# A trunk layer on one core: three spacings in the attention's side work are changed by one tick each

## The chip, the cores and the metric

The kernel runs on one core of a Trainium2 chip. TensorE (PE) multiplies matrices, VectorE (DVE) and ScalarE (ACT) work element by element, GpSimd (POOL) does the same and issues transfers of its own, and SyncE (SP) issues most of the transfers from memory. Each engine runs its own instructions in the order in which the program lists them; an instruction that needs another engine's result waits for it, and everything behind it on its engine waits too.

The metric is the device time of one execution in microseconds. Three runs of the kernel before took 2701.99, 2710.27 and 2707.65 us: median 2707.65.

## What is computed

One layer for 512 tokens of width 2048, in float32. The part that the change touches is the attention of eight heads of 128, cut from the reference:

```python
q = rmsnorm(q.reshape(B, S, SB_HEADS, SB_HEAD_DIM), q_norm_g[i])
k = rmsnorm(k.reshape(B, S, SB_HEADS, SB_HEAD_DIM), k_norm_g[i])
...
    z = jnp.einsum('bhqd,bhkd->bhqk', qi, kf).astype(jnp.float32) * scale
    strict = key_pos[None, :] < q_pos[:, None]
    log_beta = jax.nn.log_sigmoid(z)
    log_1m = jnp.where(strict, jax.nn.log_sigmoid(-z), jnp.zeros_like(z))
    tail = lax.cumsum(log_1m, axis=3, reverse=True) - log_1m
    w = jnp.where(strict, jnp.exp(log_beta + tail), jnp.zeros_like(z))
    return jnp.einsum('bhqk,bhkd->bhqd', w.astype(vf.dtype), vf)
```

So each query attends to the keys before it with weights that come from running sums along the keys. Beside this, the layer has a spatial gating, gates, an output projection, a gated feed-forward part and an embedding step; all of them are large products with weights that are read from memory once.

## The kernel before, in words

**The large products.** The layer is one long stream of matrix products, cut into units. A weight tile is loaded by SP (L316, L318), one part of it is added onto the loaded tile by a transfer that POOL issues (L338), DVE forms sums (L350), ACT rounds the result to its high half (L334) and DVE takes the low half (L331). PE multiplies with these: L271 to L273 and L629. The results are collected by ACT (L685) and DVE (L688). Weights are prepared some groups ahead.

**The side work.** Attention's small steps are put between the units. Each is a generator; a function `tick` is called about twice in each group of a product's units, and at a tick the generators that are due go on to their next `yield`. `yield n` means: go on n ticks later. `beside(steps, first)` starts a generator `first` ticks from now (1 where nothing is said). A tick only says behind which unit an instruction stands at the earliest; the scheduler that lists the instructions of each engine decides the rest by what each of them depends on. The side work's results of PE lie in a pool of two banks ("small"), so a third one must wait until the first has been read.

**The rounds.** Heads are done two at a time, in four rounds (0 to 3). In each round the loop at the end forms the queries, the keys and the values (L1238 to L1241 start their side work) and then three or four gate tiles, in whose time the attention runs. In round 0 queries, keys and values are formed together. Two halves (h = 0, 1) are the two heads.

- `q_prep` (L984): for each half, transpose (`flip`, L959), squares (L966, ACT), mean (L974, DVE), power (L976, POOL), scale (L991, DVE), then, a `yield` later, the scaling `times` (L981, ACT, four instructions) and, two ticks later, a second transpose that ACT copies out (L998).
- `k_prep` (L1001): for each half, transpose, squares, mean and power by the same lines.
- `v_prep` (L1008): for each half, transpose and `times` (L981).
- `attention` (L1013): eight blocks of 128 keys, four for each head, the last ones having 512 queries. Scores and their logarithms (`stage_a`: L1034 on PE, L1036 to L1039 on ACT), masks (`stage_m`: L1043, L1045, L1047, L1054, L1055), splitting the sums in two (`stage_b`: L1058, `stage_c`: L1062 on DVE), then the closing step of a block, `stage_d`: two products with a triangle (L1068, L1069), the sums handed on (L1071), the exponent's argument (L1073, DVE), the exponential (L1074, ACT) and the mask (L1075, POOL). `finish` (L1084 on PE) multiplies the weights of all four blocks of a head with the values, copies the output (L1086), and after the second head stores it (L1088, SP).

Of the kernel before, what the change touches and what calls it, by code (L numbers as in the profile page):

```python
# [65 lines left out]
def hybrid_layer(  # L66
# [28 lines left out]
    def nm(s):  # L95
        return f"{s}_{next(names)}"
# [14 lines left out]
    class Arena:  # L111
# [5 lines left out]
        def take(self, n, how="low"):  # L117


            spots = []  # L120
            for start, size in self.holes:
                end = start + size
                if how == "place":
                    start = -(-start // (2 * PLACE)) * 2 * PLACE
                if end - start >= n:
                    if how == "high":
                        spots.append((-end, end - n))
                    elif how != "old":
                        spots.append((start, start))
                    else:  # L130
                        spots.extend((self.given[a // P : -(-(a + n) // P)].max(), a)
                                     for a in {*range(start, end - n + 1, 256), end - n})
            at = min(spots)[1]
            start, size = next(h for h in self.holes if h[0] <= at < h[0] + h[1])
            self.holes.remove((start, size))
            self.holes.extend(
                h for h in ((start, at - start), (at + n, start + size - at - n)) if h[1])
            return Block(self, at, n)

        def give(self, block):  # L140
            self.turns += 1
            self.given[block.start // P : -(-(block.start + block.n) // P)] = self.turns
            holes = sorted(self.holes + [(block.start, block.n)])
            self.holes = holes[:1]
            for s, n in holes[1:]:
                if sum(self.holes[-1]) == s:
                    self.holes[-1] = (self.holes[-1][0], self.holes[-1][1] + n)
                else:
                    self.holes.append((s, n))
# [42 lines left out]
    def after(n, fn):  # L192
        heapq.heappush(waiting, (clock[0] + n, next(names), fn))
# [55 lines left out]
    def beside(steps, first=1):  # L249


        def step():
            n = next(steps, None)
            if n is not None:
                after(n, step)

        after(first, step)
# [595 lines left out]
    def rms_tile():  # L853
        return tmp.tile([P, 8], F32, tag="rr", name=nm("rr"), bufs=4)
# [87 lines left out]
    def a_tiles():  # L942

        for tag, n in (("l", T), ("w0", T), ("w1", 3 * P), ("w2", 2 * P), ("w3", 2 * P),
                       ("first", 5 * P), ("k", 1024), ("v", 1024), ("zs", 1024)):
            att[tag] = take(n)
        for tag in ("zh", "zl"):
            att[tag] = parts.take(T, "high")

    def a_tile(tag, n=T, start=0):  # L950
        return att[tag].f(start, start + n)
# [3 lines left out]
    def flip(o):  # L955

        ps = small_bank()
        for t in range(NT):
            nc.tensor.transpose(ps[:, t * P : (t + 1) * P], o[:, t * P : (t + 1) * P], ident)  # L959
        return ps  # L960
# [9 lines left out]
    def token_rms(ps, r):  # L970

        norm1.row()
        ms = squares(ps)
        nc.vector.scalar_tensor_tensor(out=ms, in0=ms, scalar=1.0 / P, in1=eps_cols,  # L974
                                       op0=ALU.mult, op1=ALU.add)
        nc.gpsimd.tensor_tensor(out=r, in0=ms, in1=expo[:, :NT], op=ALU.pow)  # L976

    def times(dst, ps, r):
        for t in range(NT):
            s = slice(t * P, (t + 1) * P)  # L980
            nc.scalar.activation(dst[:, s], ps[:, s], AF.Copy, scale=r[:, t : t + 1])  # L981

    def q_prep(o, i):


        for h in range(2):
            yield 2
            ps = flip(o[:, h * T : (h + 1) * T])
            q, r = take(T), rms_tile()[:, :NT]
            token_rms(ps, r)  # L990
            nc.vector.tensor_scalar(out=r, in0=r, scalar1=float(P) ** -0.5, scalar2=None,  # L991
                                    op0=ALU.mult)
            yield 1
            times(q.f(), ps, r)
            yield 2
            if not h:
                y_b[i] = take(1024)
            nc.scalar.activation(y_b[i].f(h * T, (h + 1) * T), flip(q.f()), AF.Copy,  # L998
                                 scale=gcol[:, g_q : g_q + 1])
            give(q)  # L1000
# [7 lines left out]
    def v_prep(o, v):  # L1008
        for h in range(2):
            yield 2  # L1010
            times(v[:, h * T : (h + 1) * T], flip(o[:, h * T : (h + 1) * T]), norm1.cols)

    def attention(rnd, kT, rk, v):  # L1013
# [27 lines left out]
        def stage_m(h, j):  # L1041
            l, s, w = a_tile("l")[:, : (NT - j) * P], sums(j), weights(h, j)
            nc.vector.scalar_tensor_tensor(out=w, in0=s, scalar=0.0, in1=l,  # L1043
                                           op0=ALU.min, op1=ALU.subtract)
            nc.vector.scalar_tensor_tensor(out=s, in0=s, scalar=0.0, in1=l,  # L1045
                                           op0=ALU.max, op1=ALU.add)
            nc.gpsimd.affine_select(out=s[:, :P], in_=s[:, :P], pattern=[[1, P]],  # L1047
                                    compare_op=ALU.is_gt, fill=0.0, base=0,
                                    channel_multiplier=-1)


            if j < NT - 1:
                if j:
                    nc.gpsimd.tensor_copy(first(j), s[0:1])  # L1054
                nc.gpsimd.memset(s[0:1, :P], 0.0)  # L1055

        def stage_b(j):
            nc.scalar.activation(zh[:, : (NT - j) * P], sums(j), AF.Copy)  # L1058

        def stage_c(j):  # L1060
            n = (NT - j) * P
            in_turn(nc.vector.tensor_tensor(out=zl[:, :n], in0=sums(j), in1=att["zh"].f(0, n),  # L1062
                                            op=ALU.subtract))
# [16 lines left out]
        def finish(h):  # L1080
            y = small_bank()
            for j in range(NT):
                c = h * T + j * P
                nc.tensor.matmul(y[:, j * P :], v[:, c : c + P], state.pop((h, "w", j)),  # L1084
                                 start=j == 0, stop=j == NT - 1)
            nc.scalar.activation(qT[:, h * T : (h + 1) * T], y, AF.Copy)  # L1086
            if h == 1:
                nc.sync.dma_start(out=y_spill[rnd], in_=qT)  # L1088
                give(y_b[rnd])
                y_done["b", rnd] = True  # L1090
# [7 lines left out]
        for i, (h, j) in enumerate(blocks):  # L1098
            ahead = blocks[i + 1 : i + 3]
            stage_b(j)  # L1100
            yield 1
            if i == NT:
                finish(0)
            stage_c(j)
            if ahead:
                stage_m(*ahead[0])
            yield 1
            stage_d(h, j)
            if ahead[1:]:
                stage_a(*ahead[1])  # L1110
            yield 1
# [114 lines left out]
    for n, ((w, i), pr) in enumerate(zip(order, made())):  # L1226
        if n == 0:
            row1 = norm1.row()
            nc.vector.tensor_scalar(out=eps_cols, in0=norm1.mean, scalar1=EPS, scalar2=None,
                                    op0=ALU.mult)  # L1230
        if n == 0:
            a_tiles()
        o = pr.out(block(w, i) if n < 3 else None)
        if w == "q":
            beside(q_prep(o, i))
        elif w == "k":
            kT, rk = o, rms_tile()
            beside(k_prep(kT, rk))  # L1238
            beside(attention(i, kT, rk, a_tile("v", 1024)), 6)
        elif w == "v":  # L1240
            beside(v_prep(o, a_tile("v", 1024)))  # L1241
        elif w == "s":
            scaled(o, row1)
            nc.scalar.activation(o, o, AF.Gelu_apprx_tanh)
            beside(sgu_v(i, o))
        elif w == "u":
            scaled(o, row1)
            nc.scalar.activation(o, o, AF.Gelu_apprx_tanh)
            nc.vector.tensor_tensor(out=y_a[i].f(), in0=o, in1=y_a[i].f(), op=ALU.mult)
            y_done["a", i] = True  # L1250
        else:
            d = tc.dram_tile([P, 1024], F32, name=nm("gsp"))
            nc.sync.dma_start(out=d, in_=o)
            gate_spill[w, i] = d
# [80 lines left out]
    for m in range(KH):  # L1335
        o = pair(fs, last=m == KH - 1, plain=m == 0, doubled=7).out()
# [36 lines left out]
    for j in range(KU):  # L1373
# [22 lines left out]
        else:  # L1396
            o = pair(gs, plain=j == 0).out()
# [90 lines left out]
```

## Time and profile before

| | |
|---|---|
| median of three runs | 2707.65 us (2701.99 to 2710.27) |
| the profiled execution's span | 2701.9 us |
| TensorE busy | 99% of the span |
| VectorE, ScalarE, GpSimd busy | 79%, 51%, 17% |
| memory traffic | 195 GB/s over the span |

The profile is of one execution, with all times in microseconds from the start of its span. In the list of waits a row names the engine that stood still and at what, then the engine and line that released it, then the total, how often, and the longest. In the timeline a row gives start, duration, engine, line and form, and in square brackets how long the engine was idle before it and what ended that. Matmuls overlap each other in the array, so the durations of neighbours overlap; the distance between two starts is what one takes from the stream. The clock that TensorE was granted is given as a share of full speed.

### The profile page before, as it was taken

Reading aid. Unit: us, or ns where it says so; the run is one execution under the profiler, and the core shown is the slowest. Engines: PE = TensorE matmul, PEld = TensorE weight load, DVE = VectorE, ACT = ScalarE, POOL = GpSimd, SP = SyncE. Lnnn points to the kernel's source line nnn. Section 1 sums busy time; section 2 is a strip of 40 time slices with the busy share of each in tenths; the row PEclk is TensorE's granted clock in tenths of the full one; section 3 lists DMA queues with packets and bytes.
Section 4 is the critical chain, followed back from the end, with each engine's and each line's share of the span. In section 5 each row is a group of like instructions: output and inputs, shape, how many; then the busy total and the mean of one; then the engine's idle time right before and its main releaser. Section 6 shows DMA issues by size and latency. Waiting matters only on the chain.

```text
span 2701.9 us, 43167 instructions
## 1 busy us (share of the span) xinstructions
PE 2668.1 (99%) x15875; PEld 2354.6 (87%) x15875; DVE 2147.0 (79%) x3621; ACT 1367.3 (51%) x2143; POOL 459.0 (17%) x543
## 2 busy tenths in 40 slices
PE   8999999999999999999999999999999999999999
PEld 6888888989998889988888888888888999988898
DVE  7687878787887566688988888888889667688776
ACT  7656565655554343374444444444445344453543
POOL 0232323232220000001111111111111111110110
PEclk9999999999999999999999999999999999999999
DMA  7677777777776467678888888888887668688784
GB/s 224 156 185 175 181 173 186 170 187 197 177 186 197 140 173 200 173 219 211 212 212 202 200 203 205 201 198 210 195 210 206 181 167 262 184 249 236 218 243 133
DMA packets 303268, 529.40 MB, mean 196 GB/s; under 512 B 25680, under 2 KB 162896, under 8 KB 303056
## 3 DMA queue, kind: packets, MB, share of 16 engines
q1 hardware_dynamic: 242304, 426.22, 49.9%
q0 software_dynamic: 60752, 100.43, 23.8%
q8 instruction: 124, 2.03, 0.3%
q14 instruction: 88, 0.72, 0.1%
HBM read 479.36 MB, written 47.19 MB: 195 GB/s over the span
## 4 chain that ended last, share of the span: by engine, by line
PE 88%; DVE 5%; DMA 2%; ACT 2%; issue 1%; POOL 1%; SPq 0%; DVEq 0%; ACTq 0%; POOLq 0%
PE ps L629 39%; PE ps L272 14%; PE ps L273 14%; PE ps L271 14%; PE small L629 4%; DVE wlo L331 2%; DVE out L688 1%; PE small L1084 1%; PE small L959 1%; ACT whi L334 1%; DMA wholes<-w_in 0%; DMA wholes<-w_first 0%; DVE wholes L350 0%; PE small L1034 0%; DVE parts L267 0%
## 5 line engine op out<-in xcount | busy, mean ns | idle before, releaser
L334 ACT ACTIVATE whi<-wholes 128x512 fp32r<-128x512 f32 (+4 forms) x950 | 857.6, 917 | 838.3 <-DVE wholes L350 261.9
L629 PE MATMUL ps<-parts,whi 128*128 128x512 f32 x3384 | 1134.8, 398 | 0.3 <-DVE p L688 0.3
L331 DVE TENSOR_TENSOR wlo<-wholes,whi 128x512 fp32r<-128x512 f32 (+4 forms) x950 | 962.4, 1046 | 101.0 <-ACT whi L334 100.5
L271 PE MATMUL ps<-parts,whi 128*128 128x256 f32 (+1 forms) x2675 | 855.1, 323 | 15.7 <-ACT parts L266 9.7
L272 PE MATMUL ps<-parts,whi 128*128 128x256 f32 (+1 forms) x2640 | 857.0, 325 | 1.0 <-DVE parts L267 0.8
L273 PE MATMUL ps<-parts,wlo 128*128 128x256 f32 (+1 forms) x2640 | 855.9, 325 | 0.9 <-DVE wlo L331 0.9
L629 PEld LDWEIGHTS ps<-parts,wlo 128*128 128x128 f32 x3384 | 635.8, 188 | 142.6 <-issue 1.0
L629 PE MATMUL ps<-parts,wlo 128*128 128x256 f32 x3384 | 671.1, 279 | 0.0
L271 PEld LDWEIGHTS ps<-parts,whi 128*128 128x128 f32 x2675 | 508.8, 190 | 60.7 <-ACT parts L266 10.8
L629 PEld LDWEIGHTS ps<-parts,whi 128*128 128x128 f32 x3384 | 545.3, 189 | 5.0 <-issue 1.0
L272 PEld LDWEIGHTS ps<-parts,whi 128*128 128x128 f32 x2640 | 502.7, 191 | 47.2 <-DVE parts L267 2.8
L273 PEld LDWEIGHTS ps<-parts,wlo 128*128 128x128 f32 x2640 | 502.7, 191 | 41.2 <-DVE wlo L331 2.8
L350 DVE TENSOR_TENSOR wholes<-wholes 128x256 f32<-128x256 f32 (+1 forms) x794 | 326.8, 412 | 21.8 <-DMA wholes<-w_ffn_out 4.0
L338 POOL DMA_DIRECT2D wholes<-w_ffn_in x172 | 149.7, 871 | 693.0 <-DVE wholes L350 238.8
L688 DVE TENSOR_TENSOR out<-out,ps 128x256 f32<-128x256 f32 x388 | 160.3, 415 | 131.7 <-ACT out L685 131.5
L338 POOL DMA_DIRECT2D wholes<-w_in x132 | 118.0, 895 | 486.1 <-DVE wholes L350 145.7
L655 DVE TENSOR_TENSOR out<-out 128x256 f32<-128x256 f32 x144 | 60.9, 423 | 114.7 <-ACT out L652 112.2
L629 PE MATMUL small<-parts,whi 128*128 128x512 f32 x344 | 136.5, 397 | 0.0
L267 DVE TENSOR_TENSOR parts<-wholes,parts 128x1024 fp32r<-128x1024 f32 (+4 forms) x131 | 123.7, 950 | 14.9 <-ACT parts L266 14.5
L266 ACT ACTIVATE parts<-wholes 128x1024 fp32r<-128x1024 f32 (+4 forms) x131 | 105.8, 834 | 42.0 <-DVE wholes L497 20.0
L338 POOL DMA_DIRECT2D wholes<-w_ffn_out x56 | 56.9, 1020 | 403.4 <-DMA wholes<-w_ffn_out 139.6
L1328 ACT ACTIVATE out<-out 128x512 f32<-128x512 f32 x44 | 27.8, 633 | 157.9 <-DVE out L1327 157.9
(121 smaller groups left out, 1655.0 us busy)
## 6 DMA issues: line engine op xcount, KB each, us to landing
wholes<-w_ffn_in SPq DMA_DIRECT2D x172, 384.0 KB, 5.6
wholes<-w_in SPq DMA_DIRECT2D x132, 384.0 KB, 4.9
wholes<-w_ffn_in SPq DMA_DIRECT2D x172, 256.0 KB, 4.8
wholes<-w_ffn_in POOLq DMA_DIRECT2D x172, 256.0 KB, 5.4
wholes<-w_in SPq DMA_DIRECT2D x132, 256.0 KB, 4.2
wholes<-w_in POOLq DMA_DIRECT2D x132, 256.0 KB, 5.0
wholes<-x SPq DMA_DIRECT2D x33, 512.0 KB, 5.5
wholes<-w_ffn_out SPq DMA_DIRECT2D x31, 512.0 KB, 4.5
```

Of the source, the lines that this page charges most:

```text
L266: return (nc.scalar.activation(hi, src, AF.Copy), nc.vector.tensor_tensor(out=lo, in0=src, in1=hi.bitcast(F32), op=ALU.subtract))
L267: nc.vector.tensor_tensor(out=lo, in0=src, in1=hi.bitcast(F32), op=ALU.subtract))
L271: nc.tensor.matmul(ps[:, s], sh, mh[:, s], start=start, stop=False)
L272: nc.tensor.matmul(ps, sh, ml, start=False, stop=False)
L273: return nc.tensor.matmul(ps, sl, mh, start=False, stop=stop)
L331: in_turn(nc.vector.tensor_tensor(out=self.lo[:, blocks], in0=r, in1=h.bitcast(F32), op=ALU.subtract))
L334: in_turn(nc.scalar.activation(h, r, AF.Copy))
L338: nc.gpsimd.dma_start(out=raw[:, 3:5], in_=self.src[:, 1:3], accum_op=ALU.add)
L350: in_turn(nc.vector.tensor_tensor(out=o, in0=x, in1=y, op=ALU.add))
L629: m = nc.tensor.matmul(out, l, r, start=first and k == 0, stop=last and k == 1)
L655: in_turn(nc.vector.tensor_tensor(out=out, in0=x, in1=y, op=op))
L688: in_turn(nc.vector.tensor_tensor(out=out, in0=x, in1=y, op=op))
```

## The change

Three spacings, each by one tick:

```diff
@@ q_prep
             nc.vector.tensor_scalar(out=r, in0=r, scalar1=float(P) ** -0.5, scalar2=None,
                                     op0=ALU.mult)
-            yield 1
+            yield 2
             times(q.f(), ps, r)
@@ attention
             if ahead:
                 stage_m(*ahead[0])
-            yield 1
+            yield 1 if ahead else 2
             stage_d(h, j)
@@ the loop over the tiles
         elif w == "v":
-            beside(v_prep(o, a_tile("v", 1024)))
+            beside(v_prep(o, a_tile("v", 1024)), 2)
```

- L993: in each half, the queries' scaling comes two ticks after the scale is asked for, not one. All that follows in `q_prep` moves with it: one tick for the first half's scaling and second transpose, one for the second half's first transpose, two for the second half's scaling and second transpose.
- L1107: only where no block is ahead, which is the second head's last one (j = 0), `stage_d` comes one tick later, and `finish(1)` with it.
- L1241: the values' side work starts one tick later, both halves of it.

No instruction is added or removed, and what is computed stays the same.

## The prediction

> **What bounds the kernel now.** First the page: the span, and how much of it each engine works.
>
> ```profile
> span 2701.9 us, 43167 instructions
> PE 2668.1 (99%) x15875; PEld 2354.6 (87%) x15875; DVE 2147.0 (79%) x3621; ACT 1367.3 (51%) x2143; POOL 459.0 (17%) x543
> ```
>
> PE works 2668.1 of 2701.9 us, so only some 34 us of the span can be won or lost where PE stands still; every other engine has slack on average. The same work stays after the change, and a step moved in time matters only if it takes away a wait of PE or makes one. So the second view is the list of PE's waits over the whole span (its columns: total us, how often, the longest but for the rounding).
>
> ```profile
> PE ps L271 <- ACT parts L266: 9.7, 4, 5.1
> PE small L1069 <- DVE parts L1062: 3.6, 4, 0.9
> PE small L959 <- ACT wholes L981: 2.5, 1, 2.5
> PE small L1084 <- POOL wholes L1075: 2.2, 4, 0.6
> PE small L1034 <- ACT wholes L981: 0.7, 3, 0.2
> ```
>
> The first row lies in other phases of the layer. The other four, 9.0 us together, are the small matmuls of attention, in the neighbourhood of the three edits: L1069 (second half of the closing step's product), L1084 (a head's output), L959 and L1034 (transposes and scores that wait for the scaling L981). They happen four times, once in each of the four rounds, but for the L959 row, which is round 0 alone.
>
> A wait costs more than its length if it makes the chip lower PE's clock. The timeline gives PE's gaps, and the view by stretches what follows (its columns: stretch, PE busy, then PEld, DVE, ACT and POOL with counts, granted clock, DMA share, GB/s).
>
> ```profile
> 104.03 0.85 PE L959 MATMUL small<-ident,wholes 128*128 128x128 f32 x3 [2.49 <-ACT wholes L981]
> 1179.36 0.38 PE L897 MATMUL small<-ones,wholes 128*128 128x1 f32 x2 [1.25 <-DVE wholes L887]
> 2386.54 0.50 PE L271 MATMUL ps<-parts,whi 128*128 128x512 f32 x1 [1.74 <-ACT parts L266]
> ```
>
> ```profile
> 104.10:107.50 3.40, 3.40 (x15) 3.10 (x16) 1.37 (x3) 2.82 (x11) 1.38 (x1) 0.50 0.62 184
> 107.50:109.00 1.50, 1.50 (x13) 1.45 (x13) 0.00 (x0) 0.95 (x1) 0.93 (x1) 0.99 0.06 25
> 1179.40:1182.80 3.40, 3.40 (x19) 2.97 (x20) 1.42 (x3) 3.01 (x6) 1.03 (x1) 1.00 0.93 342
> 2387.70:2391.00 3.30, 3.30 (x12) 2.72 (x11) 0.28 (x2) 0.00 (x0) 0.93 (x1) 0.50 0.75 204
> ```
>
> Behind the gap of 2.49 us the granted clock is 0.50 for 3.4 us and then 0.99; behind 1.74 us it is 0.50 too; behind 1.25 us it stays at 1.00. So a gap from somewhere between 1.25 and 1.74 us on costs a further 3.4 × 0.5 = 1.7 us. The waits of attention today, at most 0.9 us, pay none of that, except the one at 104 us.
>
> **The change part by part.** No instruction is added or removed; the built program only puts some in another order on their engines. Each part is priced by its wait.
>
> **Last block, one tick later (L1107).** One round's last block in the timeline:
>
> ```profile
> 185.45 0.39 PE L629 MATMUL ps<-parts,whi 128*128 128x512 f32 x1
> 186.02 0.68 DVE L1062 TENSOR_TENSOR parts<-wholes,parts 128x512 fp32r<-128x512 f32 x1
> 186.75 0.50 PE L1069 MATMUL small<-parts,tri 128*128 128x512 f32 x1 [0.91 <-DVE parts L1062]
> 188.60 0.41 DVE L350 TENSOR_TENSOR wholes<-wholes 128x256 f32<-128x256 f32 x1
> 188.94 0.68 DVE L1073 TENSOR_TENSOR wholes<-wholes,small 128x512 f32<-128x512 f32 x1
> 189.65 0.64 ACT L1074 ACTIVATE wholes<-wholes 128x512 f32<-128x512 f32 x1 [4.96 <-DVE wholes L1073]
> 189.87 2.18 DVE L331 TENSOR_TENSOR wlo<-wholes,whi 128x1280 fp32r<-128x1280 f32 x2
> 190.36 1.14 POOL L1075 TENSOR_SCALAR_AFFINE_SELECT wholes<-wholes 128x128 f32<-128x128 f32 x1
> 190.63 0.40 PE L629 MATMUL ps<-parts,whi 128*128 128x512 f32 x1
> 191.56 2.42 PE L1084 MATMUL small<-wholes 128*128 128x512 f32 x8 [0.53 <-POOL wholes L1075]
> ```
>
> PE's units start every 0.235 us, so L1069 was due at 185.45 + 0.24 = 185.69 and started at 186.75, behind L1062 (186.02 + 0.68 = 186.70): 1.06 us late. After the change both products stand six half units, 1.4 us, further on, where L1062 is done: the stall goes, and a slip of 0.1 in L1068 with it. −1.17 × 4 = **−4.7 us**.
>
> What is late next is finish. L1084 was due at 190.63 + 0.23 = 190.86 and began at 191.56, 0.70 late. It moves twelve units later, to about 192.3 once the stall above is out. Its chain moves further: in the built order L1073 now stands behind both L350 and both halves of L331, so it starts at about 188.60 + 2 × 0.34 + 2.18 = 191.4; L1074 follows 0.71 later (189.65 − 188.94) at 192.1, and POOL's L1075 another 0.71 later at 192.8. L1075's own length is the open one. Here it takes 1.14 us, and all of it lies beside L331 on DVE (189.87 to 192.05); elsewhere, with DVE idle beside it, it takes 0.29:
>
> ```profile
> 270.64 0.29 POOL L1075 TENSOR_SCALAR_AFFINE_SELECT wholes<-wholes 128x128 f32<-128x128 f32 x1 [0.79 <-ACT wholes L1074]
> ```
>
> With 0.3 L1084 starts at about 193.15, 0.85 late, against 0.70 now: +0.15 × 4 = **+0.6**. With 1.14 it is 1.7 late, +1.0 × 4 = +4.0. I take the short one, since L1073 now comes after that L331, and the next L331 has to wait for a load that is issued only then; the long one stays for the range.
>
> **Queries' scaling one tick later (L993), rounds 1 to 3.** The second half of the queries in round 1, and the keys behind it:
>
> ```profile
> 233.48 0.86 POOL L338 DMA_DIRECT2D wholes<-w_in  x1 [4.76 <-ACT whi L334]
> 234.04 1.62 POOL L976 TENSOR_TENSOR rr<-ms,expo 128x4 f32<-128x4 f32 x1
> 234.26 0.38 SPq L316 DMA_DIRECT2D wholes<-w_in  x1
> 235.70 0.17 DVE L991 TENSOR_SCALAR rr<-rr 128x4 f32<-128x4 f32 x1 [0.91 <-POOL rr L976]
> 235.90 1.14 ACT L981 ACTIVATE wholes<-small,rr 128x128 f32<-128x128 f32 x4 [0.85 <-DVE rr L991]
> 237.23 1.04 PE L959 MATMUL small<-ident,wholes 128*128 128x128 f32 x8
> 238.46 0.27 ACT L966 ACTIVATE sq<-small 128x128 f32<-128x128 f32 x1
> 238.85 0.28 ACT L966 ACTIVATE sq<-small 128x128 f32<-128x128 f32 x1
> 239.13 0.94 POOL L338 DMA_DIRECT2D wholes<-w_in  x1 [3.47 <-DVE wlo L331]
> 239.91 1.78 ACT L334 ACTIVATE whi<-wholes 128x1280 fp32r<-128x1280 f32 x2
> 243.06 0.60 PE L959 MATMUL small<-ident,wholes 128*128 128x128 f32 x4
> 375.74 0.92 POOL L338 DMA_DIRECT2D wholes<-w_in  x1 [4.08 <-DVE wholes L350]
> 379.03 0.60 PE L959 MATMUL small<-ident,wholes 128*128 128x128 f32 x4
> 510.44 0.92 POOL L338 DMA_DIRECT2D wholes<-w_in  x1 [2.50 <-DVE wlo L331]
> 514.99 0.60 PE L959 MATMUL small<-ident,wholes 128*128 128x128 f32 x4
> ```
>
> At 237.23 PE transposes the scaled queries and then the keys' first half, eight instructions together; at 243.06 comes the keys' second half. The edit adds a tick in each of the two halves, so the second half's transpose comes two ticks, one weight group, later: in the built order just ahead of the 243.06 one. For that its power L976 on POOL now stands behind one weight load L338 more, the one at 239.13. That load adds onto tiles which SP's transfer of 234.26 brings, and starts 4.87 us behind it; POOL, which had nothing to do for 3.47 us, waits at it, and L976 with it. L976's input is there before that: its transpose moves by one tick, half of 243.06 − 237.23, so the 234.04 of today would become about 237. So L976 starts behind the load's issue, about 239.7 (0.56 behind it, as 234.04 stands behind 233.48), ends at 241.3; L991 follows, then L981 at 241.45 for 1.14: 242.6, in time for the queries' transpose. But ACT now has the keys' four L966 (0.39 apart: 238.46, 238.85) and the two L334 (1.78) behind L981, and the keys' second transpose needs the buffer that the fourth L966 reads: the side work has two of them. 242.6 + 4 × 0.39 + 1.78 less 0.2 for overlap gives about 245.7 instead of 243.06: PE stands still for **2.6 us**. In round 2 the load starts 3.29 ahead of its transpose (375.74, 379.03) and in round 3 4.55 ahead (510.44, 514.99), against 3.93 in round 1: 3.2 and 2.0 us. Sum **+7.8**. If POOL waits for nothing there it is 0; with no weight load in the way but the later place it is at least not negative, since no wait of PE stands here today.
>
> All three gaps lie above 1.74 us, so the clock comes on top: 3 × 1.7 = **+5.1**, at the least 0.
>
> [...]
>
> The delays of DVE (L991) and ACT (L981) hide in weights prepared ahead: while the units at 237 run, L331 already makes the halves of a group some 7 us later. Without that cover each would cost its length, 0.2 and 1.1 us.
>
> **Values one tick later (L1241), and round 0.** The transposes of the values leave the place where L1034 waits for their L981 (0.7 in three waits, and some slip beside them): **−0.8**. At their new place ACT has as much in its queue; 0 to +0.3 a round, taken as nothing. In round 0 queries, keys and values come together: the second half's scaling now stands in front of the first scores, whose L1034 waits for L981 and L998, and one L1062 on DVE behind L974 and L991. Bounds: 0, and 2.5, the L959 wait that the same chain makes in round 0 (its order up to 104 us is unchanged, so that stays). I take **+1.0**, nearest to L1069's 0.9.
>
> On SP only the store of the attention's output (L1088) moves past one pair of loads, and in round 3 two small loads by one place; they are issues without a wait behind them (0.4 us of SP), covered by weights loaded well ahead. Uncovered, one load's 4.87 us.
>
> Sum: −4.7 + 0.6 + 7.8 + 5.1 − 0.8 + 1.0 = +9.0 us, against the span of 2701.9. The runs shown are 2701.99 (the profiled level), 2707.65 and 2710.27; the sum is put on their median: 2707.65 + 9.0 = **2716.6 us**.
>
> **The rivals.** **(A)** The forecast; its own range, with 0 to 2.5 for round 0 and about 1 us either way for each of the three gaps, 2709 to 2723.
>
> **(B)** Finish becomes the new stall: L1075 again takes about 1.14, because an L331 runs beside it. For it: 1.14 is its length at this very place. Against: the L331 that does it lies ahead of it now. L1084 is then 1.7 us late, at 1.74 where the clock was seen to fall. (1.0 + 1.7) × 4 = +10.8 over A: about 2727.
>
> [...]
>
> **(D)** The other side, by one mechanism: the keys' second transpose isn't held, because the load at 239.13 no longer stands in POOL's way. It decides by when that load's tiles are there: if L338 issues about 2.6 us earlier (SP's L316 sent earlier, or landing sooner than 4.87 us), the power ends by 238.7 and ACT is through by 243. Then the 7.8 and 5.1 fall away: 9.0 − 12.9 = −3.9, about 2703.7, faster. For it: the three loads vary by 1.3 us against their transposes already; against: SP's order is the same at that place.
>
> **(E)** The change does not do what it says: the order falls back to the old one, 2707.65. Against it: the built orders of PE, DVE, ACT and POOL differ at these places.
>
> **How the numbers follow.** A 0.53, B 0.10, C 0.07, D 0.20, E and what I don't see 0.10. About 0.3% (8.1 us) is what a measurement of this kernel can tell from no change: under 2699.5 faster, over 2715.8 slower. A lies over it a little more than half (0.31), B whole (0.10), and 0.06 of the rest: slower 0.47. D is faster by 0.3% only if the last block's gain is larger than reckoned or the runs scatter (0.05), and of E and the unseen 0.05: faster 0.10. Same 0.43. The range takes in D and half of B: 2702 to 2727.
>
> **What would show it.** L1069's wait gone in four rounds (−4.7). A wait of PE at L959 for ACT's L966 or L981, once in each of rounds 1 to 3, of 2.0 to 3.2 us (right), or none (D). [...] L1084's wait for L1075 near 0.85 (right) or 1.7 (B). POOL's L976 of the second half right behind a load's issue near 239.7. The forecast is wrong if PE's busy time itself changes, or if a wait for weights appears (L629 or L271 behind L331), which no term holds.

## The result, and the profile after

The changed kernel takes 2715.69 us (median of 8 runs, 2710.53 to 2721.77) against 2707.42 us for the kernel before in its 8 runs. The ratio is 1.0039, with a 95% interval of 1.0026 to 1.0053 (the two medians alone give 1.0031, inside it): slower by 7 to 14 us. The forecast was 2716.6. The number is right; the terms that it was added up from are not all right, and that is what the rest is about.

The page of the changed kernel, to be held against that of before: the busy times hardly move (PE 4.4 us more, on a span that is 14.8 us longer; a second profile of the kernel before has 3.6 us more without any edit), so most of the loss is time in which PE stands still.

```profile
span 2716.7 us, 43162 instructions
PE 2672.5 (98%) x15875; PEld 2356.0 (87%) x15875; DVE 2148.0 (79%) x3621; ACT 1367.5 (50%) x2143; POOL 463.1 (17%) x543
```

PE's waits in the attention of the changed kernel (engine, tile and line that waited, releaser, total us, times, longest; the rows of other phases are left out):

```profile
PE small L1084 <- POOL wholes L1075: 4.3, 4, 1.1
PE small L959 <- ACT sq L966: 4.0, 3, 2.0
PE small L959 <- ACT wholes L981: 2.6, 1, 2.6
PE ps L629 <- DVE out L688: 2.6, 4, 0.7
PE small L959 <- DVE wholes L1073: 1.6, 3, 0.7
PE ps L629 <- DVE p L688: 0.9, 1, 0.9
PE small L1034 <- ACT wholes L981: 0.3, 1, 0.3
PE small L1069 <- DVE parts L1062: 0.3, 1, 0.3
PE ps L629 <- DVE wlo L331: 0.2, 1, 0.2
```

L1069's wait, 3.6 us in four, is gone but for one of 0.3 that lies in round 0 on another block. Four rows are new: L959 for L966, three times; L629 for L688 with its `out`, four times; L959 for L1073, three times; L629 for L331, once. And L1084's row has doubled, from 2.2 to 4.3, and L629's wait for L688's `p`, in round 0, has grown from 0.3 to 0.9.

Two profiles of one program differ by more than some of these rows, so a common ruler is needed. The stream of large products is the same in every kernel here. The first one behind 110 us of the kernel before and the first one behind 648 us are found by counting in each trace; between them lie all four rounds of attention but the start of round 0. In these two kernels they stand here:

```profile
110.22 0.48 PE L629 MATMUL ps<-parts,whi 128*128 128x512 f32 x1
...
648.06 0.40 PE L629 MATMUL ps<-parts,wlo 128*128 128x256 f32 x2
```

```profile
111.47 0.63 PE L629 MATMUL ps<-parts,whi 128*128 128x512 f32 x2
...
659.80 0.40 PE L629 MATMUL ps<-parts,wlo 128*128 128x256 f32 x2
```

537.84 us before (648.06 − 110.22), 548.33 after: +10.5. "Distance" below always means this one, less 537.84.

### The profile page after: what moved, and what is told of

Same layout as the page of the kernel before. It is cut to its first block, busy times and chain, and to the rows that moved or that the text cites. A ratio compares the mean times of both kernels' runs of the same rounds, so it can differ in the third digit from the quotient of the medians.

```text
span 2716.7 us, 43162 instructions
## 1 busy us (share of the span) xinstructions
PE 2672.5 (98%) x15875; PEld 2356.0 (87%) x15875; DVE 2148.0 (79%) x3621; ACT 1367.5 (50%) x2143; POOL 463.1 (17%) x543
## 4 chain that ended last, share of the span: by engine, by line
PE 85%; DVE 6%; DMA 3%; ACT 2%; issue 2%; POOL 1%; SPq 0%; DVEq 0%; POOLq 0%; ACTq 0%
PE ps L629 37%; PE ps L272 14%; PE ps L271 14%; PE ps L273 14%; PE small L629 4%; DVE wlo L331 2%; DVE out L688 1%; DMA wholes<-w_in 1%; ACT whi L334 1%; DMA wholes<-x 1%; PE small L1084 1%; DVE wholes L350 1%; DMA wholes<-w_first 1%; POOL wholes L1047 0%; PE small L959 0%
## 5 line engine op out<-in xcount | busy, mean ns | idle before, releaser
L629 PE MATMUL ps<-parts,whi 128*128 128x512 f32 x3384 | 1137.1, 398 | 3.5 <-DVE out L688 2.6
L331 DVE TENSOR_TENSOR wlo<-wholes,whi 128x512 fp32r<-128x512 f32 (+4 forms) x950 | 962.5, 1046 | 108.4 <-ACT whi L334 107.9
L629 PEld LDWEIGHTS ps<-parts,wlo 128*128 128x128 f32 x3384 | 636.1, 188 | 142.8 <-issue 1.0
L629 PE MATMUL ps<-parts,wlo 128*128 128x256 f32 x3384 | 673.3, 280 | 0.2 <-DVE wlo L331 0.2
L629 PEld LDWEIGHTS ps<-parts,whi 128*128 128x128 f32 x3384 | 546.6, 189 | 10.8 <-PE small L1069 4.2
L350 DVE TENSOR_TENSOR wholes<-wholes 128x256 f32<-128x256 f32 (+1 forms) x794 | 327.7, 413 | 23.3 <-DMA wholes<-w_ffn_out 4.2
L688 DVE TENSOR_TENSOR out<-out,ps 128x256 f32<-128x256 f32 x388 | 160.2, 415 | 125.5 <-ACT out L685 125.2
L629 PE MATMUL small<-parts,whi 128*128 128x512 f32 x344 | 136.5, 397 | 0.0
```

Source lines behind the costliest of these rows:

```text
L331: in_turn(nc.vector.tensor_tensor(out=self.lo[:, blocks], in0=r, in1=h.bitcast(F32), op=ALU.subtract))
L350: in_turn(nc.vector.tensor_tensor(out=o, in0=x, in1=y, op=ALU.add))
L629: m = nc.tensor.matmul(out, l, r, start=first and k == 0, stop=last and k == 1)
L688: in_turn(nc.vector.tensor_tensor(out=out, in0=x, in1=y, op=op))
```

## The experiments

The first question was which edit costs what. Theory 1 was that each edit has the cost that the changed kernel's profile shows at its place; the rivals were the prediction's own terms.

**The kernel before once more** (no edit).

> The kernel before once more, for what two profiles of one program differ by. If the stream of products up to 104 us varies by itself, it shifts here too by up to 1.7 us, as between the two profiles at hand; from 104 to 652 us, where attention runs, it should differ by less than 0.5 us.

One run, 2707.03 us; distance +0.22. From 148 to 604 us no stage differs by more than 0.2 us; before 110 us and behind 648 us the two profiles drift apart by up to 2.7 us in one stage without any edit. So two profiles of the kernel before agree to some 0.3 us by the ruler; three of the changed kernel, at the end of this section, differ by 0.75 us without the clock's part. What the first profile of the changed kernel showed outside the ruler, 4.3 of its 14.8 us, need not be part of the change: in the two others of the same kernel it is −2.4 and +0.9.

**The queries' edit alone.**

```diff
-            yield 1
+            yield 2
             times(q.f(), ps, r)
```

> The queries' edit alone (L993). Theory 1, the terms as the changed kernel's profile shows them, each edit with its own: PE waits at L959 for ACT's L966 once in rounds 1 to 3, some 1.4, 2.3 and 1.2 us, 5 us together, and some 2 us more in round 0; the clock behind these gaps stays at 1.00; +6 to +8 us over the kernel before. Rival, the prediction's terms: gaps of 2.6, 3.2 and 2.0 us and a stretch of 3.4 us at 0.50 behind each, +13 us and more. A second rival: the gaps come only with the values' shift; then no wait at L959 here and +-1 us.

Ratio 1.0041 (1.0028 to 1.0054), distance +8.9: most of the change. Its waits have the new row:

```profile
PE small L959 <- ACT sq L966: 4.2, 3, 2.0
```

2.5 us of the 8.9 lie in round 0 (from 110 to 148 us), the rest in rounds 1 to 3. Theory 1 holds for the gaps: they come without the values' shift. It does not hold for the clock: in round 3 it was 0.50 behind a gap of 2.00 us (more on this below). That stretch costs 3.4 × 0.5 = 1.7 us and puts the run above the expected +6 to +8.

**The last block's edit alone.**

```diff
-            yield 1
+            yield 1 if ahead else 2
             stage_d(h, j)
```

> The last block's edit alone (L1107). Theory 1, from the changed kernel's profile: L1069's wait of 1.07 us goes in each round, but L629 then waits some 0.8 us for DVE's L688, which stands behind L1062, and L1084 waits some 1.5 us instead of 0.7, because L1075 takes 1.6 us beside an L331: net about +0.4 us in each round, +1.5 us in all. Rival, the prediction's terms: -1.17 and +0.15 in each round, -4.1 us in all, with L1075 at about 0.3 us and no wait of L629 for L688.

Ratio 1.0009 (0.9999 to 1.0018), distance +1.9, +0.3 to +0.6 in each round. The expected +1.5 is near; the prediction's −4.1 is excluded by the ruler. The timeline of round 0 shows why:

```profile
187.11 0.68 DVE L1062 TENSOR_TENSOR parts<-wholes,parts 128x512 fp32r<-128x512 f32 x1
188.29 0.39 PE L1069 MATMUL small<-parts,tri 128*128 128x512 f32 x1
189.32 0.47 PE L629 MATMUL ps<-parts,whi 128*128 128x512 f32 x1 [0.64 <-DVE out L688]
192.49 0.68 DVE L1073 TENSOR_TENSOR wholes<-wholes,small 128x512 f32<-128x512 f32 x1
193.21 0.64 ACT L1074 ACTIVATE wholes<-wholes 128x512 f32<-128x512 f32 x1 [0.46 <-DVE wholes L1073]
193.92 1.60 POOL L1075 TENSOR_SCALAR_AFFINE_SELECT wholes<-wholes 128x128 f32<-128x128 f32 x1 [2.16 <-ACT wholes L1074]
195.58 1.77 PE L1084 MATMUL small<-wholes 128*128 128x512 f32 x4 [1.06 <-POOL wholes L1075]
```

L1069 waits for nothing. But the L629 behind it, due 0.235 us after it at 188.53, starts at 189.32: 0.8 us late, for a result buffer that DVE's L688 empties. And L1075 takes 1.60 us, so that L1084 waits 1.06 us.

**The values' edit alone.**

```diff
-            beside(v_prep(o, a_tile("v", 1024)))
+            beside(v_prep(o, a_tile("v", 1024)), 2)
```

> The values' edit alone (L1241). Theory 1, from the changed kernel's profile: about +0.6 us in each of rounds 1 and 2 and +0.3 in round 3, since the values' transposes now stand among other side work, +1.5 us in all. Rival, the prediction's term: L1034's waits for L981 go, -0.8 us. A second rival: what stands at this place in the changed kernel comes from the queries' delay, so the edit alone gives 0.

Ratio 1.0010 (0.9999 to 1.0020), distance +1.9. L1034's wait for L981 is gone from the list, as the prediction had it, but this one has come, and the net is +0.3 to +0.5 in each round, round 0 among them:

```profile
PE small L959 <- DVE wholes L1073: 1.1, 3, 0.4
```

The values' transpose now needs the buffer that a closing step still reads. The three distances add up to 12.7, against 10.5 for all three edits; without the clock stretch in the queries' run, 11.0.

**What holds the keys' second transpose.** Theory 1: the fourth weight load ahead of the power L976 on POOL. Rival: queries' and keys' steps get in each other's way at the later place. Two kernels split the queries' edit: one gives the extra tick to the second half alone (POOL's power stays behind three loads), one to the first half alone (the second half's own spacing is the old one, but its power stands behind four loads).

```diff
-            yield 1
+            yield 2 if h else 1
             times(q.f(), ps, r)
```

> The queries' spacing for the second half only: its power L976 stays behind three weight loads on POOL in rounds 1 to 3, as in the kernel before, and only the second half's scaling and second transpose come one tick later. Theory 1 (the fourth load ahead of the power holds everything): no wait of PE at L959 for L966 over 0.3 us, and from 196 to 604 us within 0.7 us of the kernel before. Rival (the scaling and the transposes of queries and keys get in each other's way at the later place): waits at L959 of 1 to 2 us, +4 to +6 us, as with the whole edit.

```diff
-            yield 1
+            yield 1 if h else 2
             times(q.f(), ps, r)
```

> The queries' spacing for the first half only: the second half's spacing is as before, but all of it comes one tick later, and its power L976 stands behind four weight loads in rounds 1 to 3. Theory 1: PE waits at L959 for L966 or L981 by 1 to 2 us in each of rounds 1 to 3, +4 to +6 us from 196 to 604 us (and 1.7 us more for each gap that brings the clock down). Rival, as above: less than half of it, since the second half's own spacing is the old one.

Distance −0.35 with the tick in the second half alone, +6.7 with it in the first half alone (one run each, 2703.44 and 2713.03 us). The first has no wait of L959 for L966; the second waits at L959 once in each of rounds 1 to 3, for L981: there it is the queries' own second transpose, just ahead of the keys', that is held. POOL's timeline of round 1, first of the one without the wait, then of the one with it:

```profile
234.45 0.86 POOL L338 DMA_DIRECT2D wholes<-w_in  x1 [5.22 <-ACT whi L334]
235.01 1.61 POOL L976 TENSOR_TENSOR rr<-ms,expo 128x4 f32<-128x4 f32 x1
239.77 0.94 POOL L338 DMA_DIRECT2D wholes<-w_in  x1 [3.15 <-DVE wlo L331]
```

```profile
236.33 0.86 POOL L338 DMA_DIRECT2D wholes<-w_in  x1 [5.13 <-ACT sq L966]
240.72 0.88 POOL L338 DMA_DIRECT2D wholes<-w_in  x1 [3.53 <-DMA wholes<-w_in]
241.28 1.38 POOL L976 TENSOR_TENSOR rr<-ms,expo 128x4 f32<-128x4 f32 x1
```

The power comes behind one more load. POOL can only issue it when the tiles that it adds onto have landed, here 3.53 us after POOL became idle. In both kernels the second half's last transpose stands one tick later, and only the one with the load ahead of the power loses: the rival falls at this place, and the loss goes with the load. At the place two ticks later, where the whole edit puts that transpose, it was not tested without the load.

**Where the last block's stall went.** Two kernels keep queries and values as before. The first has the last block's edit and moves the second finish one tick further; the other puts the last block's L1062 on POOL besides, which changes nothing on PE, ACT and SP.

```diff
             yield 1
-        yield 1
+        yield 2
         finish(1)
```

> The last block's edit, and the second finish one tick later still; queries and values as before. Theory 1: L1084's wait for L1075 goes (1.5 us late with the last block's edit alone), L629's 0.8 us for L688 stays: -1.1 us in each round against the kernel before, -4 to -4.5 us in all. Rival: the wait follows, because L1075 and L331 come later too, and it stays at +1.5 to +2 us.

```diff
-            in_turn(nc.vector.tensor_tensor(out=zl[:, :n], in0=sums(j), in1=att["zh"].f(0, n),
-                                            op=ALU.subtract))
+            (id if last else in_turn)((nc.gpsimd if last else nc.vector).tensor_tensor(
+                out=zl[:, :n], in0=sums(j), in1=att["zh"].f(0, n), op=ALU.subtract))
...
-            stage_c(j)
+            stage_c(j, not ahead)
```

> The same, with the last block's L1062 on POOL instead of DVE. Theory 1 (L688 is late because L1062 stands ahead of it on DVE): L629's wait for L688 goes too, -0.8 us in each round against the run with L1062 on DVE, -7 to -8 us against the kernel before. Rival (L688 is late by its own chain from L685): the wait of L629 stays, and the two runs agree within 0.5 us from 110 to 604 us.

Finish later: ratio 0.9982 (0.9971 to 0.9992), distance −3.9, near the expected −4 to −4.5, L1084 without a wait, and L629's wait for L688 still 2.6 us in four. With L1062 on POOL: ratio 0.9986 (0.9976 to 0.9995), distance −5.4, and that row is gone. So L688 was late because L1062 stood ahead of it on DVE. The expected gain over the run with L1062 on DVE, 0.8 us in each round, came out as 0.1 to 0.8, 1.5 in all, so that the distance is −5.4 and not −7 to −8; what takes the rest back was not looked into. The two ratios can't tell the runs apart.

**Is the extra tick needed at all?** L1062 on POOL with the last block's spacing of before, with and without the later finish.

> The kernel before, its last block's spacing untouched, with that block's L1062 on POOL and the second finish one tick later. Theory 1 (L1062 was late only by its place on DVE: on POOL it ran 1.5 us from 181.4, long before its product is due): no wait at L1069, L629 or L1084, -1.4 to -1.9 us in each round, so as fast as the run with the last block's extra tick, -5.5 to -7.5 us against the kernel before. Rival (the extra tick is needed): L1069 still waits, -0.7 us in each round, -3 us.

> The same without the later finish. Theory 1: L1069's wait goes and L1084's grows from 0.7 to about 1.5 us, since L1073 stands where it stood on DVE: -0.2 to -0.6 us in each round. Rival (L1073 comes early with its product): L1084's wait shrinks too, -1.2 us or more in each round.

With the later finish: ratio 0.9973 (0.9962 to 0.9985), distance −5.3; no wait at L1069 or L1084, and 0.5 us once at L629 for L688. It is faster than both kernels, by about 7 us (4 to 10) against the one before, and it has none of the three edits. Without the later finish the distance is +0.1 (one run, 2698.46 us; that it lies low comes from behind 2040 us, where this profile is 6.0 us shorter than that of before). The expected −0.2 to −0.6 in each round did not come: L1069's stall is gone there too, but L1084 waits longer, 0.95 to 0.98 us in rounds 1 to 3 instead of 0.53 to 0.57, and 1.65 us in round 0. By the ruler that is +0.4 us in round 0 and 0 to −0.2 in the others. Round 0:

```profile
188.73 0.68 DVE L1073 TENSOR_TENSOR wholes<-wholes,small 128x512 f32<-128x512 f32 x1
189.44 0.63 ACT L1074 ACTIVATE wholes<-wholes 128x512 f32<-128x512 f32 x1 [4.35 <-DVE wholes L1073]
190.85 1.12 POOL L1075 TENSOR_SCALAR_AFFINE_SELECT wholes<-wholes 128x128 f32<-128x128 f32 x1
192.03 1.45 PE L1084 MATMUL small<-wholes 128*128 128x512 f32 x3 [1.65 <-POOL wholes L1075]
```

L1073 runs at 188.73 where it ran at 188.94 before: its product is done earlier, but it stands behind the same work on DVE.

**The clock behind the gaps.** Two more profiles of the changed kernel.

> The changed kernel once more, for its gaps at the keys' second transpose (1.1, 2.0 and 0.9 us in the first profile, clock 1.00 behind each). Theory 1 (the clock goes by what of a gap lies in one stretch of a fixed grid of 3.413 us, with the point near 1.6 us): the gaps of 1.1 and 0.9 us never lower the clock; the one of 2.0 us does only where over about 1.6 us of it lies between two lines of the grid. Rival (the length of the gap alone decides, as the prediction had it): the gap of 2.0 us gives the same answer each time.

> As the run before it: a third profile of the changed kernel. From 110 to 648 us both should agree with the first within 0.5 us, but for 1.7 us for a gap that lowers the clock.

One run each, 2711.00 and 2715.98 us; distances +9.8 and +11.4 beside the first profile's +10.5. Without the clock's 1.7 us the third is at +9.7, so that both lie 0.7 to 0.8 below the first, more than the expected 0.5. The gaps at the keys' second transpose in rounds 1 to 3 were 1.0, 1.7 and 1.2 us in the second, 1.4, 0.6 and 2.1 us in the third. Behind the last of these the clock was 0.50. The same wait in three runs, by the timeline and the view by stretches (stretch, busy times, granted clock, DMA share, GB/s): the changed kernel's first profile, its third, and the queries' edit alone.

```profile
387.65 0.66 PE L959 MATMUL small<-ident,wholes 128*128 128x128 f32 x4 [2.00 <-ACT sq L966]
...
387.70:391.00 3.30, 3.30 (x25) 3.12 (x26) 1.91 (x5) 3.07 (x6) 1.41 (x1) 1.00 0.50 138
```

```profile
522.78 0.66 PE L959 MATMUL small<-ident,wholes 128*128 128x128 f32 x4 [2.12 <-ACT sq L966]
...
523.60:526.80 3.20, 3.20 (x16) 3.10 (x15) 1.14 (x3) 2.50 (x4) 1.26 (x2) 0.50 0.67 204
```

```profile
522.76 1.07 PE L959 MATMUL small<-ident,wholes 128*128 128x128 f32 x4 [2.00 <-ACT sq L966]
...
522.50:522.84 0.34, 0.08 (x1) 0.09 (x2) 0.34 (x1) 0.34 (x3) 0.00 (x0) 1.00 0.04 6
522.87:523.10 0.23, 0.23 (x2) 0.23 (x3) 0.23 (x1) 0.23 (x1) 0.00 (x0) 0.50 0.00 0
522.90:526.10 3.20, 3.20 (x14) 3.00 (x14) 1.82 (x5) 1.78 (x4) 1.40 (x1) 0.50 0.53 159
```

Two gaps of exactly 2.00 us, one with the clock at 1.00 behind it, one with 0.50: length alone doesn't decide. What the traces show beside it is taken up at the end.

## Why the prediction was right, and where it was wrong

The total was right, 9.0 us forecast and about 8 to 11 measured, because errors of about 9 us on either side cancelled. That is luck. Step by step:

**The queries, rounds 1 to 3: the mechanism right, the size too large.** The chain came out as written down, instruction by instruction. Round 1 of the changed kernel:

```profile
242.24 0.88 POOL L338 DMA_DIRECT2D wholes<-w_in  x1 [3.81 <-DMA wholes<-w_in]
242.81 1.38 POOL L976 TENSOR_TENSOR rr<-ms,expo 128x4 f32<-128x4 f32 x1
244.43 1.14 ACT L981 ACTIVATE wholes<-small,rr 128x128 f32<-128x128 f32 x4 [4.05 <-DVE rr L991]
246.76 0.60 PE L959 MATMUL small<-ident,wholes 128*128 128x128 f32 x4
248.06 0.27 ACT L966 ACTIVATE sq<-small 128x128 f32<-128x128 f32 x1
248.47 0.66 PE L959 MATMUL small<-ident,wholes 128*128 128x128 f32 x4 [1.11 <-ACT sq L966]
```

POOL waits 3.81 us at the load and the power starts 0.57 us behind its issue, as reckoned; the fourth L966 releases the keys' transpose. The term of 7.8 was mis-sized: 1.1, 2.0 and 0.9 us, 4.0 in all. From the power to the transpose the sum had 6.0 us (239.7 to 245.7) and it took 5.7. The rest, 1.2 us in round 1, is PE's own time: it came to the transpose 5.1 us behind the load's issue (248.47 − 1.11 − 242.24), where the sum had taken 3.93 from the old trace. So the load came 1.2 us earlier against PE's stream than before. The traces show why: SP's transfer that it adds onto went off 0.7 us earlier against that transpose (237.90, before 234.26) and landed 3.7 us later instead of 4.2. In rounds 2 and 3 the load is 0.9 and 0.8 us earlier against the stream.

**The clock, +5.1: wrong.** "All three gaps lie above 1.74 us" failed with the sizes, and where a gap of 2.00 us came, the clock stayed up. Behind all three gaps of the changed kernel's first profile it was 1.00 (from 248.50 to 251.80, 387.70 to 391.00 and 526.00 to 529.30 us). So C, the clock that stays up, to which the prediction gave 0.07, held for that profile. It did not hold for every run: the clock was 0.50 behind 2.12 us in the third profile and behind 2.00 us in the queries' run.

**The last block, −4.7: wrong where it said that "the stall goes".** L1069's stall went in all four rounds, as forecast. What was overlooked is what stood behind it: with PE no longer held at L1069, it arrives 0.8 us early at an L629 whose buffer L688 has to empty, and L688 stands behind L1062 on DVE. The old stall had given DVE that time.

**Finish, +0.6: rival (B)'s long L1075 came, without its clock.** The reason for the short L1075, that the next L331 has to wait for a load, was wrong. The weights of the next group were there already, so an L331 started together with L1075:

```profile
195.10 0.68 DVE L1073 TENSOR_TENSOR wholes<-wholes,small 128x512 f32<-128x512 f32 x1
...
196.50 2.18 DVE L331 TENSOR_TENSOR wlo<-wholes,whi 128x1280 fp32r<-128x1280 f32 x2
196.53 1.60 POOL L1075 TENSOR_SCALAR_AFFINE_SELECT wholes<-wholes 128x128 f32<-128x128 f32 x1 [2.30 <-ACT wholes L1074]
196.73 0.40 PE L629 MATMUL ps<-parts,whi 128*128 128x512 f32 x1
198.19 1.13 PE L1084 MATMUL small<-wholes 128*128 128x512 f32 x2 [1.06 <-POOL wholes L1075]
```

L1084, due at 196.73 + 0.23, is 1.2 us late, against 0.70 before: between the forecast 0.85 and rival (B)'s 1.7. The clock behind it is 1.00 (198.20 to 201.60). Per round: −1.17 + 0.8 + 0.5, so about nothing, and +0.3 to +0.6 by the ruler, instead of −1.0. Over four rounds this step alone was 6 us off (−4.1 forecast, +1.9 measured). With the values (2.2 us off, −0.8 forecast and +1.4 measured in rounds 1 to 3) and round 0 (about 1) it is about what the clock term (5.1) and the queries' excess (3.8) were off the other way.

**The values, −0.8: wrong.** The wait left L1034 as forecast, but "taken as nothing" for the new place was +0.5 us of waiting a round at L959 in the changed kernel, and 0.35 with the values' edit alone.

**Round 0, +1.0 with bounds 0 and 2.5: inside, near the upper bound.** +1.8 to +2.3 in three profiles: L1034, L1069, L331 and above all one L629 that waits 0.9 us for L688, where it waited 0.3 before.

**Rival (D)** came by less than half: it needed the load 2.6 us earlier, and it came 0.8 to 1.2 us earlier, which made the gaps smaller and did not take them away. **Rival (E)** fell: all the moves are in the trace.

**The signs of being wrong.** The prediction named two that no term holds, a change of PE's busy time and a wait for weights. The first is 4.4 us, of which 3.6 come without any edit; the second came once, 0.2 us at L629 for L331 in round 0. Neither is large enough to change the sum.

## What to carry to other kernels

When a stall on the critical engine is removed, ask which queue used the time that the stall gave it: here DVE's evacuations did, and the stall came back as 0.8 us at the next product and 0.5 more at finish. What paid was to move the next consumer too (−3.9 us by the ruler), and the late instruction to an idle engine with it (−5.3). A side step moved by one tick is also moved in the queues of engines that look idle: POOL was busy 17% of the span, but one more load ahead of a 1.4 us power held PE for 1 to 2 us. And a total that comes out right shows little; a ruler between two fixed products, good to under 1 us, told here what ratios with intervals of ±3 us could not.

## What the runs showed of the hardware that was not expected

**Slow stretches of one length, on one grid.** In the profile of the kernel before and in the changed kernel's first, away from the program's start and end, every slow stretch has the clock at 0.50 and lasts 3.413 us by the clock record in the trace, and within a profile their starts lie a whole number of 3.4133 us apart: 104.12, 2049.72, 2387.64 and 2541.24 us before (570, 99 and 45 steps), 106.57, 2062.41, 2400.33, 2547.10 and 2564.17 after (573, 99, 43 and 5). In the queries' run one starts between 522.84 and 522.87 (rows above), and the gap of 2.00 us before it, 520.75 to 522.76, lies whole in the 3.413 us ahead. In the changed kernel's first profile one starts at 106.57, between these two rows of the view by stretches:

```profile
106.30:106.56 0.26, 0.26 (x3) 0.22 (x3) 0.23 (x2) 0.23 (x2) 0.26 (x1) 1.00 0.00 0
106.58:106.90 0.32, 0.32 (x4) 0.32 (x3) 0.28 (x2) 0.32 (x3) 0.32 (x1) 0.50 0.37 99
```

82 steps on, at 386.46, a line of the grid cuts the gap of 385.64 to 387.65 into 0.8 and 1.2 us, and the clock stays up. In the same two profiles eight gaps, four in each, have 1.74 us or more within one step of the grid (1.74 to 2.88 us), and at the end of each of these steps a slow stretch starts. Below that there are both answers: one starts at 2547.10 in the changed kernel's first profile, behind a gap of 1.13 us within one step (2545.46 to 2546.59), and none starts behind 1.22 us in the kernel before (1178.11 to 1179.32). So the prediction's point between 1.25 and 1.74 us is not one that holds, and the point near 1.6 us in the expectation for the second profile was the author's estimate, which the 1.13 us speak against. No run moved only a gap's place on the grid; what sets the clock down is not shown.

**POOL's mask beside DVE.** L1075, the same 128 x 128 instruction, took 0.29 to 0.53 us in the six places of these two profiles where DVE was idle beside it (0.29 at 270.64 before, 0.53 at 416.82 after); in the last blocks, where an L331 ran on DVE for most of it, it took 1.14 us in the kernel before (190.36) and 1.60 us in the changed one (196.53). Beside L1062 and L350 it took 0.28 to 0.36 us (0.36 at 174.96 before). No run changed only what DVE does beside it, so whether DVE's work lengthens it is not shown.
